# Where the operands of the matrix multiplications of a twelve-stage network begin in SBUF: multiples of 256 bytes for the moving ones, 64 past a multiple of 128 for the weights

## The chip, the cores and the metric

The kernel runs on one core of one Trainium2 chip. The metric is the time of one execution on the device in microseconds (us). Before the change the median of three runs is 1823.18 us (1822.3 to 1828.89).

## The reference, cut to what matters

Two small networks run one after the other on one sequence of 256 tokens of width 1024 (the first adds 16 tokens ahead, which gives 272 columns). Every stage is, in the main, `h @ w` with a large float32 weight matrix `w` that is used once:

```python
h = h + diff_attention(rms_norm(h, da_norm[j]), da_w_qkv[j], ...)      # 1024x3072, 1024x1024
h = h + conv_ffn(rms_norm(h, ffn_norm[i]), ffn_w_up[i], ...)           # 1024x5632, 2816x1024
h = h + dsa_attention(rms_norm(h, dsa_norm[j]), dsa_w_in[j], ...)      # 1024x3656, 1024x1024
...
def swiglu(h, w_gate, w_up, w_down):                                   # 1024x2816 twice, 2816x1024
    return (jax.nn.silu(h @ w_gate) * (h @ w_up)) @ w_down
```

Four such swiglu layers, a gated linear recurrence, a latent attention and two small gated embeddings make up the second network.

## The kernel before, in words

The activations lie transposed in SBUF: 1024 channels are 8 tiles of 128 partitions, and the tokens are the columns. A weight matrix is cut into blocks of 128 x 128, stored in HBM in the order of use, and read once: `load_weights` (L290) brings 16 blocks, 1 MB, in one DMA on SP's queue into one of three `raw` buffers.

A product must keep float32's precision, so every operand is split in two float32r parts, `h` (rounded) and `l` (the rest), and a block is multiplied three times (`mm3`, L336): L338 multiplies the activations' `h` by the weights' `h`, L339 `h` by the weights' `l`, L340 `l` by the weights' `h`. Eight blocks are split at a time by `weight` (L315) or, in the convolution stages, by `groups` (L798): ACT rounds `raw` into `wh` (L326, L815), DVE subtracts into `wl`. These tiles come from the pool `spl`, four buffers each.

In almost all products the block of weights is the stationary operand (loaded by an LDWEIGHTS instruction) and the activations are the moving one, with 272 columns (stage da, conv0 and most of dsa), 258 (the rest of dsa, conv1's first product) or 256 (all that follows). In a few (`proj_n`, L373) it is the other way round: the weights move, 512 columns wide, and 128 columns of the activations are loaded.

The moving operands are tiles of one row of 8 or 22 blocks per partition. `operand` (L488) makes most of them (`xh` and `xl` from the pool `res`, `hh` and `hl` between the two products of a feed-forward layer). The attention stages have `oh` and `ol`, the recurrence `mof`, `mok`, `moml` and `mob`, the latent attention `ch`, `cl` and the tiles `q0` to `q7` and `c0` to `c7`.

Where these begin in a partition follows from the order in which the pools lay them out. In the program that is built from the kernel before:

| tiles | columns | bytes past a multiple of 256 |
|---|---|---|
| all `wh`, `wl` (8 buffers, 4096 bytes apart) | | 64 |
| `xh`, `xl` of every stage, block 0 | 272, 258, 256 | 160 |
| the same, blocks 1 to 7, 272 columns (1088 bytes a block) | 272 | 224, 32, 96, 160, ... |
| the same, 258 columns (1032 bytes a block) | 258 | 168, 176, ... 216 |
| the same, 256 columns (1024 bytes a block) | 256 | 160 |
| `oh`, `ol` of da; `hh`, `hl` of conv0 (1088 bytes a block) | 272 | 0, 64, 128, 192 in turn |
| `hh`, `hl` of conv1, glu00, glu01, glu10; `ph`, `pl` of ple0 | 256 | 128 |
| `hh`, `hl` of glu11 | 256 | 192 |
| `mof`, `mok`, `mob`; `moml`; `ch`, `cl` | 256 | 64; 128; 96 |

The stages run in this order, and their two products follow each other on TensorE without a break: da 7 to 165 us, conv0 165 to 372, dsa 372 to 554, conv1 554 to 746, glu00 746 to 943, even 943 to 1071, glu01 1071 to 1259, ple0 1259 to 1301, glu10 1301 to 1493, mla 1493 to 1598, glu11 1598 to 1788, ple1 to the end. In a feed-forward stage the first two thirds multiply `xh`, `xl`, the last third `hh`, `hl`.

The order of the instructions on each engine is planned by the framework from priorities (`EARLIER`, L195); in the convolution stages and in dsa's attention it is written out by hand.

Of the kernel before, what the change touches and what calls it, by code (L numbers as in the profile page):

```python
# [9 lines left out]
F32 = mybir.dt.float32  # L10
F32R = mybir.dt.float32r
# [9 lines left out]
TA = 272  # L21
TB = 256

NQ = NM - 2
TQ = TA - NQ
KD = 8
FT = 22
G = 16
GS = 8
# [152 lines left out]

TAGS = {"ru": "t0", "s": "t0", "rv": "t1", "z": "t1", "d": "t1", "ra": "t2", "rb_": "t2", "vt": "t3", "sq": "t4",
# [21 lines left out]
def part(f):  # L205

    @wraps(f)
    def moved(self, *a, **k):
        with self.earlier(f.__name__):
            return f(self, *a, **k)  # L210
    return moved


class Net:
# [36 lines left out]
    def t_(self, shape, dt=F32, tag="t", pool=None):  # L251
        self.nt += 1
        pool = pool or self.tmp
        name = f"{tag}_{self.nt}"
        if pool is self.tmp:
            tag = TAGS.get(tag, tag)
        bufs = {"bufs": BUFS[tag]} if pool is self.tmp and tag in BUFS else {}
        return pool.tile(shape, dt, name=name, tag=tag, **bufs)
# [55 lines left out]

    @part  # L315
    def weight(self, n=1):
        nc = self.nc
        i = self.pos % G
        if i == 0:
            self.load_weights()  # L320
        if i in self.cuts:
            self.at, g = i, min(self.cuts[i], self.left)
            raw = self.raw[:, i * 128:(i + g) * 128]
            h = self.t_([128, GS * 128], F32R, "wh", self.spl)
            l = self.t_([128, GS * 128], F32R, "wl", self.spl)
            nc.scalar.copy(out=h[:, :g * 128], in_=raw)  # L326
            self.tt(l[:, :g * 128], raw, h[:, :g * 128].bitcast(F32), OP.subtract)
            self.cur = (h, l)
        self.pos += n
        self.left -= n  # L330
        s = slice((i - self.at) * 128, (i - self.at + n) * 128)
        if i + n == G:
            self.cuts = {j: GS for j in range(0, G, GS)}
        return self.cur[0][:, s], self.cur[1][:, s]
# [153 lines left out]
    def operand(self, kt, T, tag="x", pool=None):  # L488

        ts = [self.t_([128, kt, T], F32R, tag + c, pool or self.res) for c in "hl"]  # L490
        return [[t[:, k] for k in range(kt)] for t in ts]
# [141 lines left out]
    def diff_attention(self, scope):  # L633
# [35 lines left out]
        o = [pool.tile([128, KD, TA], F32R, name=n) for n in ("oh", "ol")]  # L669
# [134 lines left out]
    def groups(self, key):  # L804

        self.begin(key)
        n = self.left
        for i in range(0, n, GS):
# [4 lines left out]
            h = self.t_([128, GS * 128], F32R, "wh", self.spl)  # L813
            l = self.t_([128, GS * 128], F32R, "wl", self.spl)
# [97 lines left out]
    def dsa(self, scope):  # L912
# [19 lines left out]
        o = [pool.tile([128, KD, TQ], F32R, name=n) for n in ("oh", "ol")]  # L932
# [11 lines left out]
        rk = self.t_([128, TA], F32, "rk")  # L944
# [7 lines left out]
        kn = self.t_([128, TA], F32, "kn")  # L952
        ks = self.t_([128, TA], F32, "ks")
# [19 lines left out]
        def index(i):  # L973
            q0, qn = QT[i + 1]
            nk = q0 + qn
            sc = pool.tile([128, TA], F32, name=f"sc{i}")[:, :nk]
            for h in range(8):
# [5 lines left out]
                else:  # L983
                    rl = self.t_([128, TA], F32, "rl")[:, :nk]
# [345 lines left out]
    def even(self, scope):  # L1330
# [5 lines left out]
        big = lambda n, dt=F32: pool.tile([128, W], dt, name=n)  # L1336
# [187 lines left out]
        for part, tags in zip(mo, (("f", "k"), ("ml", "b"))):  # L1524
            for tag in tags:
                t = pool.tile([128, 4, TB], F32R, name=f"mo{tag}", tag=tag)
                part += [t[:, i] for i in range(4)]
# [73 lines left out]
    def mla(self, scope):  # L1601
# [26 lines left out]
        for m, p in enumerate(self.projs(x, KD, TB, 6, 3)):  # L1628
            self.section("c")
            t = self.t_([128, TB], F32, f"c{m}", pool)  # L1630
# [117 lines left out]
        def queries(h):  # L1748
# [5 lines left out]
            qT[h] = self.t_([128, TB], F32, f"q{h}", pool)  # L1754
# [54 lines left out]
        def outputs(h, aT):  # L1809
# [5 lines left out]
            o[0].append(self.t_([128, TB], F32R, f"q{h}", pool))  # L1815
            o[1].append(self.t_([128, TB], F32R, f"c{h}", pool))
# [124 lines left out]
```

## Time and profile before

| | |
|---|---|
| median of 3 runs | 1823.18 us |
| the profiled execution: its time, its span | 1823.16 us, 1821.4 us |
| busy share of the span: PE, DVE, ACT, POOL | 98%, 70%, 53%, 17% |
| mean granted clock of TensorE | 0.988 of full speed |
| DMA | 296 MB, 162 GB/s on average |

PE is TensorE, PEld its weight loads, DVE VectorE, ACT ScalarE, POOL GpSimd. The span is the time from the first to the last instruction of the profiled execution. A matmul's record lasts about 0.28 us, and the next one begins long before its end, so PE shows as busy throughout; what a matmul costs in a row of equal ones is the distance from one start to the next, called its pitch here. From a table of stretches it is (length + 0.28 us) / count, as every record that reaches into the stretch is counted.

### The profile page before, as it was taken

How to read it: one execution, taken by the hardware profiler on the slowest of the kernel's cores; microseconds unless marked ns; L12 is line 12 of the kernel's file. 1: busy time of each engine (PE TensorE's matmuls, PEld its weight loads, DVE VectorE, ACT ScalarE, POOL GpSimd, SP SyncE). 2: the span in 40 equal slices, each digit the busy share in tenths (PEclk: the TensorE clock that was granted, in tenths of full speed). 3: DMA queues.
4: the chain of work that ended last, by engine and by line, in shares of the span. 5: the costliest groups of instructions: out<-in, count | busy, mean ns of one | idle time of the engine just before them, and what ended most of it. 6: DMA issues, size and time to landing. Idle time of an engine off the chain costs nothing.

```text
span 1821.4 us, 34478 instructions
## 1 busy us (share of the span) xinstructions
PE 1780.2 (98%) x13982; PEld 1698.2 (93%) x13982; DVE 1283.1 (70%) x2294; ACT 964.8 (53%) x1664; POOL 303.9 (17%) x301
## 2 busy tenths in 40 slices
PE   8999999999999999999999999999899999999998
PEld 7889999998779999899997799999899998899997
DVE  7776887578567986666678876666866679676666
ACT  4444877433356875444446554445554447654444
POOL 1202443112103441300013210001300014000001
PEclk9999999999899999999999999999999999999999
DMA  7323355454304555455554245555355553255552
GB/s 242 120 101 139 140 185 186 169 183 159 130 27 160 186 187 191 155 186 185 185 200 149 96 174 185 186 185 191 139 182 185 184 186 122 94 192 180 180 184 87
DMA packets 51151, 295.90 MB, mean 162 GB/s; under 512 B 6832, under 2 KB 15152, under 8 KB 16688
## 3 DMA queue, kind: packets, MB, share of 16 engines
q1 hardware_dynamic: 50992, 293.70, 45.6%
q8 instruction: 110, 1.80, 0.4%
q14 instruction: 49, 0.40, 0.1%
HBM read 287.56 MB, written 1.05 MB: 158 GB/s over the span
## 4 chain that ended last, share of the span: by engine, by line
PE 92%; DVE 3%; POOL 2%; ACT 2%; issue 1%; DMA 0%; SPq 0%; DVEq 0%; ACTq 0%; POOLq 0%
PE acc L338 27%; PE acc L340 27%; PE acc L339 27%; PE t L504 2%; PE s L588 1%; PE s L1432 1%; DVE wl L249 1%; POOL sacc L249 1%; POOL lv L249 1%; PE s L1786 1%; PE s L980 0%; PE o L620 0%; PE s L339 0%; PE t L478 0%; PE s L340 0%
## 5 line engine op out<-in xcount | busy, mean ns | idle before, releaser
L249 DVE TENSOR_TENSOR wl<-raw,wh 128x1024 fp32r<-128x1024 f32 (+1 forms) x541 | 677.1, 1253 | 263.2 <-ACT wh L326 255.8
L326 ACT CAST wh<-raw 128x1024 fp32r<-128x1024 f32 (+1 forms) x453 | 473.1, 1046 | 579.4 <-PE acc L340 392.8
L339 PE MATMUL acc<-xh,wl 128*128 128x256 f32 (+2 forms) x2632 | 751.9, 286 | 5.2 <-DVE wl L249 5.1
L338 PE MATMUL acc<-xh,wh 128*128 128x256 f32 (+2 forms) x2632 | 754.4, 287 | 2.6 <-ACT xh L395 2.3
L340 PE MATMUL acc<-xl,wh 128*128 128x256 f32 (+2 forms) x2632 | 753.6, 287 | 0.0
L338 PEld LDWEIGHTS acc<-xh,wh 128*128 128x128 f32 x2632 | 499.7, 190 | 7.5 <-ACT xh L395 3.0
L339 PEld LDWEIGHTS acc<-xh,wl 128*128 128x128 f32 x2632 | 499.3, 190 | 7.3 <-DVE wl L249 6.1
L340 PEld LDWEIGHTS acc<-xl,wh 128*128 128x128 f32 x2632 | 497.3, 189 | 1.1 <-DVE xl L396 0.4
L340 PE MATMUL acc<-hl,wh 128*128 128x256 f32 (+1 forms) x1056 | 296.6, 281 | 0.0
L339 PE MATMUL acc<-hh,wl 128*128 128x256 f32 (+1 forms) x1056 | 296.3, 281 | 0.0
L338 PE MATMUL acc<-hh,wh 128*128 128x256 f32 (+1 forms) x1056 | 296.1, 280 | 0.0
L249 POOL TENSOR_TENSOR sacc<-sacc,sq 128x256 f32<-128x256 f32 (+2 forms) x96 | 99.0, 1032 | 1109.5 <-ACT sq L445 1071.3
L338 PEld LDWEIGHTS acc<-hh,wh 128*128 128x128 f32 x1056 | 198.5, 188 | 0.0
L340 PEld LDWEIGHTS acc<-hl,wh 128*128 128x128 f32 x1056 | 198.3, 188 | 0.0
L339 PEld LDWEIGHTS acc<-hh,wl 128*128 128x128 f32 x1056 | 198.3, 188 | 0.0
L249 POOL TENSOR_TENSOR y<-y,z 128x272 f32<-128x272 f32 (+1 forms) x88 | 109.5, 1244 | 162.8 <-ACT z L866 161.6
L815 ACT CAST wh<-raw 128x1024 fp32r<-128x1024 f32 x88 | 91.3, 1038 | 20.2 <-PE acc L340 20.2
L864 ACT ACTIVATE y<-u,cols 128x272 f32<-128x272 f32 (+1 forms) x88 | 53.5, 608 | 53.7 <-DVE u L249 53.4
L249 DVE TENSOR_TENSOR s<-s,acc 128x256 f32<-128x256 f32 x88 | 36.7, 421 | 46.8 <-PE acc L340 45.6
L396 DVE SCALAR_TENSOR_TENSOR xl<-x,cols,xh 128x256 fp32r<-128x256 f32 (+2 forms) x80 | 64.0, 808 | 6.8 <-ACT xh L395 6.8
L395 ACT ACTIVATE xh<-x,cols 128x256 fp32r<-128x256 f32 (+2 forms) x80 | 39.9, 507 | 29.1 <-DVE x L249 28.6
L249 DVE TENSOR_TENSOR hl<-s,hh 128x256 fp32r<-128x256 f32 (+1 forms) x132 | 55.2, 421 | 0.0
(504 smaller groups left out, 2195.3 us busy)
## 6 DMA issues: line engine op xcount, KB each, us to landing
raw<-wts SPq DMA_DIRECT2D x268, 1024.0 KB, 4.8
x<-xT SPq DMA_DIRECT2D x8, 136.0 KB, 4.4
k<-ra SPq DMA_DIRECT2D x16, 68.0 KB, 2.0
raw<-wts SPq DMA_DIRECT2D x2, 512.0 KB, 4.8
out<-xn SPq DMA_DIRECT2D x4, 256.0 KB, 2.0
raw<-wts SPq DMA_DIRECT2D x3, 256.0 KB, 3.6
q<-ra SPq DMA_DIRECT2D x8, 68.0 KB, 2.1
q<-ra SPq DMA_DIRECT2D x8, 64.5 KB, 2.0
```

What stands on the lines that cost most here:

```text
L249: (eng or self.nc.vector).tensor_tensor(out=out, in0=a, in1=b, op=op)
L326: nc.scalar.copy(out=h[:, :g * 128], in_=raw)
L338: mm(out, a[0], b[0], start=first, stop=False)
L339: mm(out, a[1], b[0], start=False, stop=False)
L340: mm(out, a[0], b[1], start=False, stop=last)
L395: nc.scalar.mul(out=h, in_=src, mul=scale)
L396: nc.vector.scalar_tensor_tensor(out=l, in0=src, scalar=scale, in1=h.bitcast(F32), op0=OP.mult, op1=OP.subtract)
L504: self.nc.tensor.transpose(out, in_, self.ident[:n, :n])
L588: self.nc.tensor.matmul(out, q[ps, q0:q0 + qn], k[ps, :q0 + qn], start=True, stop=False)
L815: self.nc.scalar.copy(out=h, in_=raw)
L864: nc.scalar.activation(out=y, in_=u[:, 2:], func=AF.Identity, scale=tap(n, 2), bias=self.col("conv_b", 44 * layer + 22 * (n % 2) + n // 2))
L1432: nc.tensor.matmul(p[:, i], ke[:, c], qe[:, c], start=True, stop=True)
```

## The change

It adds a constant `LINE = 256` and places the tiles by it. The tiles of moving activations begin on a multiple of 256 bytes, and the blocks in them are padded to a multiple of 256 bytes: with 272 or 258 columns a block takes 1280 bytes in place of 1088 or 1032, with 256 it stays at 1024. The weight tiles get 16 unused columns ahead of their 1024, and an alignment of 128 bytes, so that the data begin 64 bytes past a multiple of 128. In dsa four small tiles (`rk`, `kn`, `ks`, `rl`) move from the shared pool `tmp` to pools of the stage; `rk` and `ks` share the buffers of the score tiles `sc0` and `sc1`. The instructions, their number and their sizes stay.

In dsa some products begin inside a block (`off` in `projs`, L351): the index heads at column 16, the queries at column 14. Those columns keep their distance of 64 and 56 bytes from the block's start. The 512 wide moving operands of `proj_n` are weights and lie where those lie.

```diff
+LINE = 256
...
+def lines(n):
+
+    return -(-n * 4 // LINE) * LINE // 4
...
-    def t_(self, shape, dt=F32, tag="t", pool=None):
+    def t_(self, shape, dt=F32, tag="t", pool=None, line=None):
...
+        if line:
+            bufs["align_bytes"] = line
         return pool.tile(shape, dt, name=name, tag=tag, **bufs)
...
+    def halves(self):
+
+        q = LINE // 16
+        return [self.t_([128, q + GS * 128], F32R, "w" + c, self.spl, LINE // 2)[:, q:] for c in "hl"]
+
...
-            h = self.t_([128, GS * 128], F32R, "wh", self.spl)
-            l = self.t_([128, GS * 128], F32R, "wl", self.spl)
+            h, l = self.halves()
...
-        ts = [self.t_([128, kt, T], F32R, tag + c, pool or self.res) for c in "hl"]
-        return [[t[:, k] for k in range(kt)] for t in ts]
+        ts = [self.t_([128, kt, lines(T)], F32R, tag + c, pool or self.res, LINE) for c in "hl"]
+        return [[t[:, k, :T] for k in range(kt)] for t in ts]
...
-        o = [pool.tile([128, KD, TA], F32R, name=n) for n in ("oh", "ol")]
+        o = [pool.tile([128, KD, lines(TA)], F32R, name=n, align_bytes=LINE)[:, :, :TA] for n in ("oh", "ol")]
...
-        rk = self.t_([128, TA], F32, "rk")
+        rk = pool.tile([128, TA], F32, name="rk", tag="sc0")
...
-        kn = self.t_([128, TA], F32, "kn")
-        ks = self.t_([128, TA], F32, "ks")
+        kn = pool.tile([128, TA], F32, name="kn")
+        ks = pool.tile([128, TA], F32, name="ks", tag="sc1")
...
-            sc = pool.tile([128, TA], F32, name=f"sc{i}")[:, :nk]
+            sc = pool.tile([128, TA], F32, name=f"sc{i}", tag=f"sc{i}")[:, :nk]
...
-                    rl = self.t_([128, TA], F32, "rl")[:, :nk]
+                    rl = self.t_([128, TA], F32, "rl", wk)[:, :nk]
...
-        big = lambda n, dt=F32: pool.tile([128, W], dt, name=n)
+        big = lambda n, dt=F32: pool.tile([128, W], dt, name=n, align_bytes=LINE)
...
-                t = pool.tile([128, 4, TB], F32R, name=f"mo{tag}", tag=tag)
+                t = pool.tile([128, 4, TB], F32R, name=f"mo{tag}", tag=tag, align_bytes=LINE)
...
-            o[0].append(self.t_([128, TB], F32R, f"q{h}", pool))
-            o[1].append(self.t_([128, TB], F32R, f"c{h}", pool))
+            o[0].append(self.t_([128, TB], F32R, f"q{h}", pool, LINE))
+            o[1].append(self.t_([128, TB], F32R, f"c{h}", pool, LINE))
```

The tiles `oh`, `ol` of dsa change as those of da do, `c0` to `c5` and `q0` to `q7` of the latent attention as the last lines shown, and `groups` calls `halves` as `weight` does.

## Rows read from the trace of the kernel before

**Rows 1.** The page, part 1: busy time of each engine.

```profile
PE 1780.2 (98%) x13982; PEld 1698.2 (93%) x13982; DVE 1283.1 (70%) x2294; ACT 964.8 (53%) x1664; POOL 303.9 (17%) x301
```

**Rows 2.** The page, part 4: the chain that ended last, by engine, by line.

```profile
PE 92%; DVE 3%; POOL 2%; ACT 2%; issue 1%; DMA 0%; SPq 0%; DVEq 0%; ACTq 0%; POOLq 0%
PE acc L338 27%; PE acc L340 27%; PE acc L339 27%; PE t L504 2%; PE s L588 1%; PE s L1432 1%; DVE wl L249 1%; POOL sacc L249 1%; POOL lv L249 1%; PE s L1786 1%; PE s L980 0%; PE o L620 0%; PE s L339 0%; PE t L478 0%; PE s L340 0%
```

**Rows 3.** PE's groups by form: line, op, tiles, form, count, busy us, mean ns.

```profile
L338 PE MATMUL acc<-xh,wh 128*128 128x256 f32 x1560 | 441.4, 283 | 2.3 <-ACT xh L395 2.3
L338 PE MATMUL acc<-hh,wh 128*128 128x256 f32 x880 | 245.6, 279 | 0.0
...
L338 PE MATMUL acc<-xh,wh 128*128 128x272 f32 x656 | 194.5, 297 | 0.3 <-ACT le L659 0.3
...
L338 PE MATMUL acc<-xh,wh 128*128 128x258 f32 x416 | 118.5, 285 | 0.0
...
L338 PE MATMUL acc<-hh,wh 128*128 128x272 f32 x176 | 50.5, 287 | 0.0
L338 PE MATMUL acc<-wh,xh 128*128 128x512 f32 x96 | 39.2, 409 | 0.0
...
L338 PE MATMUL acc<-oh,wh 128*128 128x272 f32 x64 | 18.7, 292 | 0.0
...
L338 PE MATMUL acc<-oh,wh 128*128 128x258 f32 x64 | 18.4, 287 | 0.0
...
L338 PE MATMUL s<-xh,wh 128*128 128x256 f32 x40 | 11.4, 286 | 0.0
...
L338 PE MATMUL s<-xh,wh 128*128 128x272 f32 x24 | 7.2, 319 | 2.7 <-ACT wh L326 2.7
```

**Rows 4.** Table of stretches in which TensorE has one kind of product.

```profile
core 0: us, PE busy (x) PEld busy (x) DVE busy (x) ACT busy (x) POOL busy (x), PEclk, DMA share, GB/s
235.00:285.00 50.00, 50.00 (x401) 50.00 (x400) 40.15 (x68) 38.46 (x68) 25.05 (x17) 1.00 0.53 187
310.00:370.00 60.00, 60.00 (x480) 60.00 (x480) 32.65 (x36) 26.84 (x35) 6.83 (x6) 1.00 0.47 168
640.00:680.00 40.00, 40.00 (x333) 40.00 (x333) 32.52 (x56) 30.78 (x55) 18.65 (x14) 1.00 0.52 180
690.00:744.00 54.00, 54.00 (x461) 54.00 (x460) 30.58 (x35) 25.82 (x35) 6.04 (x6) 1.00 0.52 186
...
1080.00:1195.00 115.00, 115.00 (x959) 114.95 (x959) 74.39 (x111) 56.35 (x83) 0.00 (x0) 1.00 0.52 184
1202.00:1258.00 56.00, 56.00 (x497) 56.00 (x496) 35.48 (x42) 26.97 (x35) 6.83 (x6) 1.00 0.54 191
...
1433.00:1490.00 57.00, 57.00 (x486) 57.00 (x485) 35.12 (x43) 26.04 (x34) 7.11 (x6) 1.00 0.53 185
...
1728.00:1786.00 58.00, 58.00 (x491) 58.00 (x491) 35.06 (x42) 26.50 (x35) 6.12 (x6) 1.00 0.52 182
```

**Rows 5.** PE in order of time where glu01 passes from xh to hh.

```profile
1198.06 0.28 PE L340 MATMUL acc<-xl,wh 128*128 128x256 f32 x1
...
1198.90 0.28 PE L338 MATMUL acc<-hh,wh 128*128 128x256 f32 x1
...
1199.47 0.28 PE L340 MATMUL acc<-hl,wh 128*128 128x256 f32 x1
```

**Rows 6.** What PE waited for, longest first.

```profile
PE t L478 <- DVE dg L249: 6.5, 3, 2.8
```

**Rows 7.** The page, part 5: how the weights are split.

```profile
L249 DVE TENSOR_TENSOR wl<-raw,wh 128x1024 fp32r<-128x1024 f32 (+1 forms) x541 | 677.1, 1253 | 263.2 <-ACT wh L326 255.8
L326 ACT CAST wh<-raw 128x1024 fp32r<-128x1024 f32 (+1 forms) x453 | 473.1, 1046 | 579.4 <-PE acc L340 392.8
```

**Rows 8.** The instructions of dsa's tiles rk and sc.

```profile
L955 DVE SCALAR_TENSOR_TENSOR kn<-ki,cols,rk x1: 494/494/494, 394.7 to 394.7; 64x272 f32<-64x272 f32 x1
...
L982 DVE TENSOR_SCALAR sc<-s,wi x2: 367/434/501, 405.2 to 428.8; 128x144 f32<-128x144 f32 x1, 128x272 f32<-128x272 f32 x1
```

More of the change, by code (lines that the diff above doesn't have):

```diff
@@ L812, in groups @@
             raw = self.raw[:, i % G * 128:(i % G + GS) * 128]
-            h = self.t_([128, GS * 128], F32R, "wh", self.spl)
-            l = self.t_([128, GS * 128], F32R, "wl", self.spl)
+            h, l = self.halves()
             self.nc.scalar.copy(out=h, in_=raw)
@@ L931, in dsa @@
         vn = pool.tile([128, 3, 1024], F32, name="vn")
-        o = [pool.tile([128, KD, TQ], F32R, name=n) for n in ("oh", "ol")]
+        o = [pool.tile([128, KD, lines(TQ)], F32R, name=n, align_bytes=LINE)[:, :, :TQ] for n in ("oh", "ol")]
         self.section()
@@ L1629, in mla @@
             self.section("c")
-            t = self.t_([128, TB], F32, f"c{m}", pool)
+            t = self.t_([128, TB], F32, f"c{m}", pool, LINE)
             self.tt(t, p, r, OP.mult)
@@ L1753, in queries @@
                 pss[g] = self.sps([128, 2, 4])
-            qT[h] = self.t_([128, TB], F32, f"q{h}", pool)
+            qT[h] = self.t_([128, TB], F32, f"q{h}", pool, LINE)
             nc.vector.tensor_copy(out=qT[h], in_=p)
```

## The prediction, made before the changed kernel was run

> **What bounds the kernel.** I read the busy times first: PE is busy 98% of the span, DVE 70%, ACT 53% [rows 1]. The chain that ended last says the same in another way: 92% of it is PE, and 81% is the three lines of `mm3` [rows 2]. The longest wait of PE on another engine is 6.5 us in total [rows 6]. So the time is the number of matmuls times the pitch from one to the next, and a change counts only by what it does to the pitch.
>
> Next, how many there are [rows 3]. Each row stands for one line of `mm3` and so for a third. 256 columns: 1560 + 40 and 16 more in mla's lead tile, 1616 a line or 4848 on `xh`, `xl`; 880 a line or 2640 on `hh`, `hl`; by the plan of weights another 168 a line or 504 in the small groups (`ev_o` 64, `ml_o` 64, `pp0` 16, 24 of `ml_n`). 272 columns: 656 + 176 + 64 + 24 = 920 a line, 2760. 258 columns: 480 a line, 1440. 512 columns: 96 a line and a few more, where the weights move.
>
> Then the pitch, from stretches with a single kind of product [rows 4], as (length + 0.28) / count. With 256 columns on `xh`, 160 bytes past a multiple of 256: 115.28 / 959 = 120.2 ns. On `hh` at 128 bytes: conv1 54.28 / 461 = 117.7, glu10 57.28 / 486 = 117.9, but glu01 56.28 / 497 = 113.2. On `hh` at 192 bytes, glu11: 58.28 / 491 = 118.7. With 272 columns: 125.4 on conv0's `xh`, at odd multiples of 32 bytes, and 125.6 on its `hh`, which runs through 0, 64, 128 and 192. With 258 columns and steps of 8 bytes: 121.0. These rows have a granted clock of 1.00, which is the higher level, 2.4 GHz, so the clock explains none of the differences; nor does a wait, as PE has no idle time in any of them. Instruction, shape and weights' offset (64 past a multiple of 128) are the same. What differs is where the moving operand begins, and in glu01 against glu10 not even that (both at 128): two pitches exist for one placement. At the seam inside glu01 it can be seen to switch: seven steps on `xh` take 0.84 us, 120 ns each, the next five on `hh` 0.57 us, 114 each [rows 5].
>
> **The change, part by part.** *Weights.* They lie 64 past a multiple of 128 before and after, so this part removes nothing; the larger tiles only make half of them 192 in place of 64 past a multiple of 256. No row has that. Bounds: nothing, or the 1.0 ns between 117.7 and the 118.7 of glu11, where moving operand and weights differ by 128 bytes instead of 64; I take nothing.
>
> *256 columns on `xh`.* From 160 to 0 past 256. No row shows 0 with 256 columns; the nearest are those at 128, which are whole multiples of 128 too: 113.2 at one end, 117.8 at the other. All rows at 128 but one are at the upper end, but those came in from a stage at 160, and glu01 stayed at the lower one for all its stretch. I can't tell which of the two a stage takes, so I take half: 115.5. 4848 x (120.2 - 115.5) = 22.8 us. (The 96 of dsa's index heads begin 64 past a multiple of 256 after the change too; they are 0.4 us of it.) A loss is the last rival below.
>
> *256 columns on `hh`.* From 128 to 0: 1584 (conv1, glu00, glu10) x (117.8 - 115.5) = 3.6 us; glu01 loses 528 x (115.5 - 113.2) = 1.2; glu11 gains 528 x (118.7 - 115.5) = 1.7. Together 4.1.
>
> *The 504 others.* No clean stretch of them; between nothing and the 4.6 ns from 117.8 to 113.2. At half, 1.2 us.
>
> *272 columns.* Padding puts every block at 0. Priced by columns: 115.5 x 272 / 256 = 122.7, against 125.5 now: 2760 x 2.8 = 7.7 us; bounds 120.3 (from 113.2) and 125.2 (from 117.8).
>
> *258 columns.* 115.5 x 258 / 256 = 116.4 against 121.0, for 1248, as 192 (dsa's queries, from column 14) stay 56 bytes past: 5.7 us. Bounds 114.1 and 118.7.
>
> *512 columns.* The moving side stays at 64 past 128: nothing, either way at most the 4.6 ns per 256 columns, 3 us.
>
> *dsa's four tiles.* `rk` now shares a buffer with `sc0`, so the first write to `sc0` waits for the last reader of `rk`. That reader starts at 394.7, that write at 405.2 [rows 8]: 10 us of cover. Were it gone, DVE would stand 0.5 us, and ACT's `rl` and POOL's select behind it. `ks` and `sc1` have 30 us. `rl` keeps two buffers. Nothing. No DMA and no queue is moved.
>
> *The other engines.* DVE and ACT write the same elements; no row says that their 1253 and 1046 ns [rows 7] depend on the place, so nothing. They hide behind PE: in glu01's first product DVE works 74.4 of 115 us, and if PE needs 110 it is at 67%. What is late next is DVE in conv0's first product, 40.2 of 50 us [rows 4], 84% at the fastest pitch.
>
> Sum: 22.8 + 4.1 + 1.2 + 7.7 + 5.7 = 41.5 us. PE is 92% of the chain [rows 2], the rest isn't shortened: 38 us. The profiled execution took 1823.2 us (span 1821.4), 0.02 from the median, so **1785**.
>
> **The rivals.**
> *All fall into the fast pitch.* 113.2, 120.3 and 114.1: 4848 x 7.0 + 1584 x 4.6 + 528 x 5.5 + 504 x 4.6 + 2760 x 5.2 + 1248 x 6.9 = 33.9 + 7.3 + 2.9 + 2.3 + 14.4 + 8.6 = 69 us, at 92% 64: 1759. For it: glu01, and that now all operands lie alike, so that nothing throws a stage out of it. Against: three of four stages at 128.
>
> *All take the slower aligned pitch.* 117.8, 125.2, 118.7: 4848 x 2.4 - 528 x 4.6 + 528 x 0.9 + 2760 x 0.3 + 1248 x 2.3 = 11.6 - 2.4 + 0.5 + 0.8 + 2.9 = 13.4, at 92% 12: 1811. For it: the same three rows.
>
> *The place doesn't matter.* The pitches would then be those of how the stages happen to start, and come out as now, 1823. Against: every clean stretch on `xh` has 120, every one at 128 less. The Trainium skill (SBUF — State Buffer, "Who interferes with whom") says that PE waits on nobody and reads moving operand and weights through two independent ports; by it this change does nothing, and 1823 is its time. The trace speaks against a pitch that nothing but the width sets: 113.2, 117.8 and 120.2 for one form [rows 4].
>
> *Slower: 0 collides.* A moving operand at 0 may meet weights at 64 and 192 alternately, and never settle; every 256-wide matmul then costs the 120.2 of `xh`, and 272 columns 127.7 by columns. The xh groups stay, `hh` loses 1584 x 2.4 + 528 x 7.0 + 528 x 1.5 = 8.3, the others 504 x 2.4 = 1.2, the 272 wide 2760 x 2.2 = 6.1: 15.6, at 92% 14: 1837. It decides from a mean pitch that is 0.8 ns above today's over some 12,000 matmuls (9 us). For it: with 272 columns the tiles at 0, 64, 128 and 192 are no better than those at 32 [rows 4].
>
> **How the numbers follow.** The middle course 0.34, all fast 0.28, all slower-aligned 0.16, no effect 0.14, slower 0.08. Half a per cent, 9 us, is about what a measurement of this kernel can tell from no change. Faster by more: the first two and three quarters of the third, 0.74; within: 0.18; slower: 0.08. The range goes from the all fast case to the slower-aligned one with a few us at each end for the 512 wide and the unknown place of weights: 1755 to 1816.
>
> **What would show it.** The stretches on `xh` in glu00 to glu11: 120.2 now, 113 to 118 if I am right, one value for a whole stage. The stretches on `hh` should no longer differ from `xh` of the same stage. conv0 should go from 125.5 to 120 to 123. The counts, DVE's and ACT's means and PE's waits should stay. Wrong it would be if `xh` stays at 120, or if PE's idle time grows by what its pitch saves.

## The result, and the profile after

The changed kernel takes 1783.9 us (median of 5 runs, 1783.2 to 1787.12); the kernel before, timed beside it, 1826.32 us (5 runs, 1822.3 to 1828.89). The ratio is 0.9774, 95% interval 0.9755 to 0.9793. Executions of one kernel differ by up to some 14 us, the longer ones at a lower mean granted clock (the change run once more: 1779.2 us at 0.989, 1793.5 at 0.981). The profiled execution has a span of 1782.2 us against 1821.4, so 39.2 us less. 1785 had been predicted; how the terms fared is another matter.

Parts 1 and 4 of the page of the kernel after: busy times, and the chain that ended last by engine and by line.

```profile
PE 1739.4 (98%) x13982; PEld 1658.8 (93%) x13982; DVE 1282.5 (72%) x2294; ACT 964.3 (54%) x1664; POOL 300.7 (17%) x301
...
PE 90%; DVE 4%; POOL 2%; ACT 2%; issue 1%; DMA 0%; SPq 0%; DVEq 0%; ACTq 0%; POOLq 0%
PE acc L352 26%; PE acc L353 26%; PE acc L354 26%; PE t L518 2%; DVE wl L257 1%; PE s L602 1%; PE s L1445 1%; POOL sacc L257 1%; PE s L1799 1%; POOL lv L257 1%; PE s L993 0%; PE o L634 0%; PE s L353 0%; PE s L354 0%; PE s L1798 0%
```

Against [rows 1, 2]: as many instructions on every engine, and PE is the one whose busy time falls by much, 1780.2 to 1739.4. The chain still belongs to `mm3`, which is now L352 to L354.

The table of stretches of the kernel after, in the order conv0 `xh`, conv0 `hh`, conv1 `xh`, conv1 `hh`, glu01 `xh`, glu01 `hh`, glu11 `xh`, glu11 `hh`. The clean stretches have moved up with the stages, so they aren't those of [rows 4] to the microsecond.

```profile
core 0: us, PE busy (x) PEld busy (x) DVE busy (x) ACT busy (x) POOL busy (x), PEclk, DMA share, GB/s
235.00:285.00 50.00, 50.00 (x402) 50.00 (x401) 40.57 (x68) 38.86 (x68) 24.90 (x17) 1.00 0.51 182
310.00:370.00 60.00, 60.00 (x482) 60.00 (x482) 33.16 (x37) 26.79 (x36) 6.89 (x7) 1.00 0.48 169
640.00:680.00 40.00, 40.00 (x334) 40.00 (x333) 33.13 (x57) 30.94 (x55) 18.03 (x14) 1.00 0.51 179
690.00:740.00 50.00, 50.00 (x444) 50.00 (x443) 29.85 (x33) 24.53 (x33) 6.08 (x6) 1.00 0.56 196
...
1072.00:1175.00 103.00, 103.00 (x911) 103.00 (x910) 70.37 (x99) 53.66 (x80) 0.00 (x0) 1.00 0.54 193
1183.00:1238.00 55.00, 55.00 (x488) 55.00 (x487) 35.01 (x42) 26.30 (x35) 6.52 (x6) 1.00 0.55 192
...
1575.00:1685.00 110.00, 110.00 (x971) 109.95 (x970) 74.56 (x109) 56.87 (x83) 0.00 (x0) 1.00 0.55 193
1695.00:1745.00 50.00, 50.00 (x444) 50.00 (x443) 32.35 (x39) 24.28 (x33) 5.50 (x6) 1.00 0.56 197
```

With 256 columns all have one pitch. The second products of conv1 and glu11 have 50.28 / 444 = 113.2 ns, before 117.7 and 118.7; glu01's second has 55.28 / 488 = 113.3, before 113.2; glu01's first has 103.28 / 911 = 113.4, before 120.2. The 110.28 / 971 = 113.6 of glu11's first takes in a short gap at 1578 us. With 272 columns next to nothing has changed: 50.28 / 402 = 125.1 and 60.28 / 482 = 125.1, for 125.4 and 125.6. With 258 columns nothing: 40.28 / 334 = 120.6 for 121.0. The granted clock is 1.00 in all of them, before and after.

PE in order of time at the seam inside glu01, as in [rows 5], but after:

```profile
1180.02 0.28 PE L352 MATMUL acc<-xh,wh 128*128 128x256 f32 x1
...
1180.36 0.28 PE L352 MATMUL acc<-hh,wh 128*128 128x256 f32 x1
...
1180.93 0.28 PE L354 MATMUL acc<-hl,wh 128*128 128x256 f32 x1
```

Three steps on `xh` take 0.34 us and five on `hh` 0.57: 113 and 114 ns. The switch from 120 to 114 that stood there is gone.

What stayed, as [rows 6, 7] (waits of PE, part 5 of the page):

```profile
PE t L492 <- DVE dg L257: 7.0, 3, 2.9
...
L257 DVE TENSOR_TENSOR wl<-raw,wh 128x1024 fp32r<-128x1024 f32 (+1 forms) x541 | 676.6, 1252 | 250.3 <-ACT wh L340 243.2
L340 ACT CAST wh<-raw 128x1024 fp32r<-128x1024 f32 (+1 forms) x453 | 473.0, 1046 | 537.5 <-PE acc L354 364.3
```

The splitting of the weights costs 1252 and 1046 ns as before, and PE's longest wait is 7.0 us for 6.5.

Summed over the whole trace, from each matmul's start to the next one's, by the width of the first (summed over all 13,981 distances; the pitch is the mean without the gaps at seams):

| columns | matmuls | before, us | after, us | pitch before, after, ns |
|---|---|---|---|---|
| 256 | 7,992 | 964.9 | 924.2 | 118.9, 113.6 |
| 272 | 2,760 | 376.8 | 377.4 | 125.4, 125.1 |
| 258 | 1,440 | 176.4 | 176.3 | 120.5, 120.5 |
| 512 | 378 | 103.4 | 104.6 | 233.9, 231.1 |
| others | 1,411 | 190.2 | 189.9 | |

The products of 256 columns save 40.7 us; all else together gives back 1.4, so 39.3 in all, the span's 39.2.

### The profile page after: what moved, and what is told of

The parts are those of the page before. It is cut to its first block, busy times and chain, and to the rows that moved or that the text cites. A ratio compares the mean times of both kernels' runs of the same rounds, so it can differ in the third digit from the quotient of the medians.

```text
span 1782.2 us, 34479 instructions
## 1 busy us (share of the span) xinstructions
PE 1739.4 (98%) x13982; PEld 1658.8 (93%) x13982; DVE 1282.5 (72%) x2294; ACT 964.3 (54%) x1664; POOL 300.7 (17%) x301
## 4 chain that ended last, share of the span: by engine, by line
PE 90%; DVE 4%; POOL 2%; ACT 2%; issue 1%; DMA 0%; SPq 0%; DVEq 0%; ACTq 0%; POOLq 0%
PE acc L352 26%; PE acc L353 26%; PE acc L354 26%; PE t L518 2%; DVE wl L257 1%; PE s L602 1%; PE s L1445 1%; POOL sacc L257 1%; PE s L1799 1%; POOL lv L257 1%; PE s L993 0%; PE o L634 0%; PE s L353 0%; PE s L354 0%; PE s L1798 0%
## 5 line engine op out<-in xcount | busy, mean ns | idle before, releaser
L257 DVE TENSOR_TENSOR wl<-raw,wh 128x1024 fp32r<-128x1024 f32 (+1 forms) x541 | 676.6, 1252 | 250.3 <-ACT wh L340 243.2
L340 ACT CAST wh<-raw 128x1024 fp32r<-128x1024 f32 (+1 forms) x453 | 473.0, 1046 | 537.5 <-PE acc L354 364.3
L352 PE MATMUL acc<-xh,wh 128*128 128x256 f32 (+2 forms) x2632 | 747.1, 284 | 2.9 <-ACT xh L409 2.6
L354 PE MATMUL acc<-xl,wh 128*128 128x256 f32 (+2 forms) x2632 | 744.2, 283 | 0.0
L352 PEld LDWEIGHTS acc<-xh,wh 128*128 128x128 f32 x2632 | 499.9, 190 | 7.4 <-ACT xh L409 3.0
L354 PEld LDWEIGHTS acc<-xl,wh 128*128 128x128 f32 x2632 | 498.7, 190 | 0.8
L352 PE MATMUL acc<-hh,wh 128*128 128x256 f32 (+1 forms) x1056 | 293.9, 278 | 0.0
L354 PE MATMUL acc<-hl,wh 128*128 128x256 f32 (+1 forms) x1056 | 293.6, 278 | 0.0
L352 PEld LDWEIGHTS acc<-hh,wh 128*128 128x128 f32 x1056 | 198.6, 188 | 0.0
L354 PEld LDWEIGHTS acc<-hl,wh 128*128 128x128 f32 x1056 | 198.3, 188 | 0.0
```

The source lines that it names most:

```text
L257: (eng or self.nc.vector).tensor_tensor(out=out, in0=a, in1=b, op=op)
L352: mm(out, a[0], b[0], start=first, stop=False)
L354: mm(out, a[0], b[1], start=False, stop=last)
```

## The experiments

Two questions: why does every product of 256 columns now have 113.3 ns, and why did those of 272 and 258 not move? The first theory was the prediction's own: a moving operand on a multiple of 128 or 256 bytes can have either of two pitches, whatever the weights. Its rivals: the distance from weights to moving operand decides; the history decides, that is, a stage keeps the pitch in which it starts. Pitches below are those of a clean stretch at clock 1.00; the columns of all tables are those of the one above. Places are bytes past a multiple of 256.

One fact of the changed program belongs here. With 64 bytes ahead of the data a weight buffer is 4224 bytes instead of 4096, so four buffers begin in turn at 64 and at 192. Before, all began at 64.

### Many places, weights as in the change

`operand` gets an offset by stage:

```diff
+OFF = {('conv1', 'h'): 128, ('glu00', 'x'): 128, ('glu00', 'h'): 64, ('glu01', 'x'): 64, ('glu01', 'h'): 192,
+       ('glu10', 'x'): 32, ('glu10', 'h'): 160, ('glu11', 'x'): 16, ('glu11', 'h'): 96}
-        ts = [self.t_([128, kt, lines(T)], F32R, tag + c, pool or self.res, LINE) for c in "hl"]
-        return [[t[:, k, :T] for k in range(kt)] for t in ts]
+        q, n = OFF.get((self.stage, tag), 0) // 4, lines(T)
+        ts = [self.t_([128, kt * n + q], F32R, tag + c, pool or self.res, LINE) for c in "hl"]
+        return [[t[:, q + k * n:q + k * n + T] for k in range(kt)] for t in ts]
```

> The changed kernel, with the moving operands of single products pushed off their multiple of 256 bytes, weights as in the change (64 or 192 past). conv1's hh at 128 and glu00's xh at 128; glu00's hh and glu01's xh at 64; glu01's hh at 192; glu10's xh at 32 and its hh at 160; glu11's xh at 16 and its hh at 96. Theory 'place against weights' (whole multiples of 128 don't meet weights at 64 past 128): 113 ns at 128 as at 0, about 118.7 at 64 and 192 as in glu11 before, about 120 at 32, 160, 96 and 16. Theory 'multiples of 256 alone': 113 nowhere but at 0, 117.8 at 128. Theory 'history' (a stage of whole multiples of 64 takes either pitch, as the one before left it): no order by place, 113 or 118 at 128, 64 and 192 alike.

One run, 1816.5 us. Stretches of conv1 `hh` (128), glu00 `hh` (64), glu01 `hh` (192), glu11 `xh` (16):

```profile
690.00:740.00 50.00, 50.00 (x443) 50.00 (x443) 29.50 (x33) 24.52 (x33) 6.08 (x6) 1.00 0.54 191
...
875.00:932.00 57.00, 57.00 (x481) 57.00 (x480) 34.75 (x41) 25.82 (x35) 6.16 (x6) 1.00 0.52 185
...
1190.00:1248.00 58.00, 58.00 (x489) 58.00 (x488) 35.65 (x43) 26.00 (x34) 6.08 (x6) 1.00 0.51 182
...
1600.00:1715.00 115.00, 115.00 (x968) 114.95 (x968) 74.27 (x107) 56.59 (x84) 0.00 (x0) 1.00 0.52 184
```

128 has 113.5 ns, as 0 has; 64 has 119.1, 192 119.2, 16 119.1. By the same reading 32 and 160 have 119.2 and 119.1, and 96 has 118.1. So a change of place within the pair 0 and 128 costs nothing, everything else 5 to 6 ns. That 64 and 192, whole multiples of 64, are as bad as 16 speaks for a relation to the weights, which lie at just these two places. A stage that follows a slow one was fast again where its place was 0, so history alone doesn't decide here.

### Many places, all weights at 0

```diff
-        q = LINE // 16
-        return [self.t_([128, q + GS * 128], F32R, "w" + c, self.spl, LINE // 2)[:, q:] for c in "hl"]
+        return [self.t_([128, GS * 128], F32R, "w" + c, self.spl, LINE) for c in "hl"]
...
+OFF = {('conv1', 'h'): 64, ('glu00', 'h'): 64, ('glu01', 'x'): 64, ('glu10', 'x'): 128, ('glu10', 'h'): 192,
+       ('glu11', 'x'): 32, ('glu11', 'h'): 96}
...
```

Here and in the runs below with an `OFF`, `operand` takes the offsets as in the first run.

> The weights' part undone and set the other way: all weights on a multiple of 256, moving operands at 0 (glu00's xh, glu01's hh, all of even, ple, mla), 64 (conv1's hh, glu00's hh, glu01's xh), 128 (glu10's xh), 192 (glu10's hh), 32 and 96 (glu11). Theory 'difference' (only the distance between moving operand and weights counts, 64 past 128 is good): the moving operands at 64 and 192 have 113 ns, those at 0 and 128 some 118.7. Theory 'the weights' place doesn't count': 113 at 0 as after the change, the rest as in the run with weights at 64. In both, 120 at 32 and 96.

One run, 1816.23 us. conv1 `hh` (64), glu01 `hh` (0), glu10 `hh` (192):

```profile
690.00:740.00 50.00, 50.00 (x427) 50.00 (x426) 28.62 (x32) 23.59 (x33) 6.01 (x6) 1.00 0.53 190
...
1195.00:1250.00 55.00, 55.00 (x461) 55.00 (x460) 33.30 (x40) 24.38 (x32) 5.39 (x5) 1.00 0.50 175
...
1432.00:1485.00 53.00, 53.00 (x470) 53.00 (x469) 34.34 (x41) 25.04 (x33) 7.10 (x6) 1.00 0.55 197
```

0 over weights at 0 is now among the worst, 55.28 / 461 = 119.9; 64 has 117.8, and 192 has 113.4. By the same reading 128 has 118.8, 32 has 116.9 and 96 has 120.2. The very place that the change gives to every moving tile is among the worst with other weights: the theory that the place of the moving operand alone decides is out. But the distance alone isn't enough: weights at 64 or 192 and moving at 0 are 192 or 64 apart, and here 192 apart is fast, 64 apart is not.

### Other widths at the place of the change

The two products of the four swiglu layers at widths of 240 to 320, each beginning at 0, weights as in the change. Wider ones read on into the next block, and what lies beyond 256 is dropped; glu11 computes only the first 240 tokens.

```diff
+WIDE = {"00": (272, 288), "01": (258, 264), "10": (320, 304), "11": (240, 240)}
...
-        ps = self.projs(x, KD, TB, 2 * FT, 4)
+        ps = (p[:, :N] for p in self.projs(self.wide(x, WIDE[key][0]), KD, WIDE[key][0], 2 * FT, 4))
...
-            p = self.proj(h, FT, TB)
+            p = self.proj(self.wide(h, WIDE[key][1]), FT, WIDE[key][1])[:, :N]
```

> All places as in the change; only the number of moving columns differs: glu00 272 on xh and 288 on hh, glu01 258 and 264, glu10 320 and 304, glu11 240 and 240 (the surplus columns come from the next block and are dropped, the last block repeats the one before it; in glu11 the last 16 tokens are left out of the layer). Theory 'so much a column' (0.443 ns a column, as 113.3 for 256): 240 at 106, 258 at 114, 264 at 117, 272 at 120, 288 at 127.5, 304 at 134.6, 320 at 141.7; then conv0's 125 would come from something else in that stage. Theory 'width must be a multiple of 64 columns (256 bytes)': 320 at 141.7, the others dear, 0.461 to 0.467 ns a column: 258 at 120.5, 272 at 125, 288 at 133, 304 at 141. Theory 'multiple of 16 columns': 240, 272, 288, 304, 320 at 0.443, 258 and 264 dear.

One run, 1863.68 us. 272, 258, 264, 320 and 240 columns:

```profile
770.00:880.00 110.00, 110.00 (x882) 110.00 (x881) 67.77 (x97) 50.61 (x76) 0.00 (x0) 1.00 0.50 174
...
1082.00:1203.00 121.00, 121.00 (x1008) 120.94 (x1007) 78.55 (x118) 58.91 (x87) 0.19 (x1) 1.00 0.53 186
1210.00:1268.00 58.00, 58.00 (x484) 58.00 (x483) 34.76 (x41) 26.13 (x35) 6.78 (x6) 1.00 0.51 182
1330.00:1465.00 135.00, 135.00 (x929) 134.95 (x928) 72.87 (x103) 54.39 (x82) 0.00 (x0) 1.00 0.42 149
...
1655.00:1765.00 110.00, 110.00 (x982) 109.95 (x981) 74.92 (x114) 55.94 (x83) 0.00 (x0) 1.00 0.56 198
```

| columns | 240 | 256 (in the change) | 258 | 264 | 272 | 288 | 304 | 320 |
|---|---|---|---|---|---|---|---|---|
| pitch, ns | 112.3 | 113.2 to 113.6 | 120.3 | 120.4 | 125.0 | 131.8 | 139.6 | 145.6 |
| columns at 2.4 GHz, ns | 100.0 | 106.7 | 107.5 | 110.0 | 113.3 | 120.0 | 126.7 | 133.3 |
| above that | 12.3 | 6.6 to 6.9 | 12.8 | 10.4 | 11.7 | 11.8 | 12.9 | 12.3 |

From 240 to 320 columns a column costs (145.6 - 112.3) / 80 = 0.416 ns, one period of 2.4 GHz. The second line is width / 2.4, the third the difference. Seven widths pay 10 to 13 ns over their columns and 256 alone pays 7, at the same place and over the same weights. At its slow pitches, 117.8 to 120.0, 256 columns pay 11 to 13 as well. None of the theories had this: of the eight widths only 256 has the cheap pitch here, and two columns more cost 7 ns. Whether 240, 264, 288, 304 or 320 columns have a cheap pitch at other places was not run; 272 and 258 had none at any of the places that were run (about 125 and 119 ns at best).

### Everything at 128

```diff
+OFF = {('conv1', 'h'): 128, ('glu00', 'x'): 128, ('glu00', 'h'): 128, ('glu01', 'x'): 128, ('glu01', 'h'): 128,
...
```

> All moving operands of 256 columns that the helper makes (xh, hh, ph, ch) at 128 past a multiple of 256, as hh was before; the rest as in the change. Theory 'place against weights': as fast as the change, 1784. Theory 'multiples of 256 alone': the 7,500 matmuls cost 117.8 in place of 113.5, 1784 + 32 = 1816. Theory 'history' (the xh at 160 ahead threw the stages on hh out of the fast pitch): 1784 too, with single stages at 117.8 possible.

1786.05 us (4 runs, 1783.8 to 1788.39), ratio to before 0.9794 (0.9778 to 0.981). glu01 `xh`:

```profile
1065.00:1175.00 110.00, 110.00 (x970) 109.85 (x968) 76.40 (x114) 56.75 (x84) 0.00 (x0) 1.00 0.55 195
```

110.28 / 970 = 113.7 ns, and the intervals overlap with the change's. With weights by turns at 64 and 192, a multiple of 128 does as well as one of 256.

### The change without its weights

```diff
-        q = LINE // 16
-        return [self.t_([128, q + GS * 128], F32R, "w" + c, self.spl, LINE // 2)[:, q:] for c in "hl"]
+        return [self.t_([128, GS * 128], F32R, "w" + c, self.spl) for c in "hl"]
```

In this program the plain weight tiles come to lie at 0.

> The weights' part undone, the moving operands as in the change: plain tiles of 4096 bytes, which then lie on multiples of 256 (all at 0). By the run with weights at 0 each matmul of 256 columns costs 120.0 ns, and the time is 1784 + 7,900 x (120.0 - 113.6) = 1834, slower than before (1822). Theory 'the moving operands alone bring it': 1784.

1832.82 us (5 runs, 1831.14 to 1836.14), ratio 1.0046 (1.0028 to 1.0063). conv1 `hh`, glu01 `xh`:

```profile
690.00:740.00 50.00, 50.00 (x419) 50.00 (x419) 27.22 (x32) 23.61 (x31) 4.83 (x5) 1.00 0.52 184
...
1075.00:1185.00 110.00, 110.00 (x918) 109.95 (x917) 72.01 (x108) 53.68 (x81) 0.99 (x1) 1.00 0.54 188
```

50.28 / 419 = 120.0 and 120.1 ns, and by the same reading 119.9 in glu00's second product: everything at the slow end. The aligned and padded moving operands by themselves make the kernel slower than before, by 0.3 to 0.6%.

### The weights alone

Weights as in the change; `xh`, `hh`, `ph` and `ch` back to the places of before (160, 128 or 192, 128, 96), and no padding. The recurrence's tiles, `q` and `c` stay as in the change.

```diff
-    return -(-n * 4 // LINE) * LINE // 4
+    return n
...
+OFF = {('glu00', 'x'): 160, ('glu01', 'x'): 160, ('glu10', 'x'): 160, ('glu11', 'x'): 160, ('conv1', 'h'): 128,
+       ('glu00', 'h'): 128, ('glu01', 'h'): 128, ('glu10', 'h'): 128, ('glu11', 'h'): 192,
...
```

> The weights' part alone: weights at 64 and 192 by turns, moving operands where they lay before (xh at 160, hh at 128, in glu11 192, ph 128, ch 96, no padding); mo, q and c as in the change. Theory 'the turns': hh at 128 goes to 113.4 in conv1, glu00 and glu10 (1584 x 4.4 = 7 us), xh at 160 to 119.2 (4848 x 0.9 = 4 us), some 1 us in the small groups: about 1810. Theory 'history': hh stays at 117.8 behind xh at 160, about 1817. Theory 'the moving operands alone bring it': 1822.

1815.71 us (10 runs, 1807.21 to 1822.0), ratio 0.9948 (0.9928 to 0.9968). glu00 `hh` (128), glu01 `xh` (160):

```profile
880.00:935.00 55.00, 55.00 (x487) 55.00 (x486) 34.85 (x42) 26.28 (x35) 6.20 (x6) 1.00 0.55 192
1070.00:1188.00 118.00, 118.00 (x991) 117.95 (x990) 78.17 (x118) 58.34 (x86) 0.00 (x0) 1.00 0.53 187
```

`hh` at 128 has 55.28 / 487 = 113.5 right behind an `xh` at 160 with 119.4. In the kernel before, conv1 and glu10 had 117.7 and 117.9 for the same `hh` at the same place, behind the same `xh` [rows 4]. All four products of `hh` at 128 were fast here, conv1, glu01 and glu10 at 113.5, 113.4 and 113.8. What differs is that half of the weights lie at 192. So with weights by turns a slow stage ahead doesn't hold the next one at the slow pitch: there the theory of history falls. Whether it falls with one place for all weights too, this run can't tell.

### All weights at 64

One place for all weights, several for the moving tiles, no padding:

```diff
+OFF = {('glu01', 'x'): 128, ('glu01', 'h'): 128, ('glu10', 'x'): 160, ('glu10', 'h'): 128, ('glu11', 'h'): 128}
...
-    return -(-n * 4 // LINE) * LINE // 4
+    return n
...
-        return [self.t_([128, q + GS * 128], F32R, "w" + c, self.spl, LINE // 2)[:, q:] for c in "hl"]
+        return [self.t_([128, q + GS * 128 + 48], F32R, "w" + c, self.spl, LINE)[:, q:q + GS * 128] for c in "hl"]
```

> All eight weight tiles at 64 past a multiple of 256, as before the change, in place of 64 and 192 by turns; blocks of 272 and 258 columns without padding; moving operands at 0 on conv1's hh, all of glu00, even and glu11's xh, at 128 on glu01's xh and hh, at 160 then 128 in glu10 (the order of before), at 0 then 128 in glu11. Theory 'the turns' (64 and 192 in turn lead every stage into the fast pitch; with all at 64 a stage can stay in the slow one): 117.8 on most of the stages at 0 or 128, whatever stood ahead. Theory 'history': 113.4 in all of them but glu10's hh, which follows operands at 160 and stays at 117.8. Theory 'distance by 256' (64 behind the weights is good, 64 ahead is not): 113.4 on all at 0, 117.8 on all at 128.

One run, 1810.99 us. glu00 `hh` (0), glu01 `hh` (128), glu11 `xh` (0):

```profile
880.00:928.00 48.00, 48.00 (x426) 48.00 (x426) 31.38 (x37) 22.96 (x32) 6.19 (x6) 1.00 0.55 195
...
1188.00:1243.00 55.00, 55.00 (x470) 55.00 (x469) 34.60 (x41) 24.93 (x33) 6.09 (x6) 1.00 0.54 189
1600.00:1712.00 112.00, 112.00 (x953) 112.00 (x952) 73.51 (x105) 54.93 (x83) 0.00 (x0) 1.00 0.54 187
```

At 0, 48.28 / 426 = 113.3 in glu00 but 112.28 / 953 = 117.8 in glu11: two pitches for one placement in one run, as in the kernel before. At 128, 117.6.

### Few columns loaded

If the slow pitch comes from the reading of the moving operand meeting the loading of the next weights, a shorter load should cost less. In the second products of the swiglu layers only the first 64, 64, 32 and 128 output channels of each block of 128 are computed, the rest is left out.

```diff
+LOADED = {"00": 64, "01": 64, "10": 32, "11": 128}
+OFF = {('glu00', 'h'): 64, ('glu01', 'x'): 64, ('glu10', 'h'): 64, ('glu11', 'x'): 64, ('glu11', 'h'): 64}
...
-            self.mm3(p[:, :T], self.weight(), (x[0][k], x[1][k]), k == 0, k == kt - 1)
+            self.mm3(p[:M, :T], [w[:, :M] for w in self.weight()], (x[0][k], x[1][k]), k == 0, k == kt - 1)
...
```

> Weights as in the change; in the second product of the swiglu layers only a part of the 128 weight columns is loaded (glu00 and glu01 64, glu10 32, glu11 all 128), so the rest of the layer's output is left out. Moving operands at 64 on xh of glu01 and glu11 and on hh of glu00, glu10 and glu11, at 0 on hh of glu01. Theory 'the moving read meets the load of the next weights': fewer columns loaded, fewer meetings, so glu00's hh (at 64, 64 columns loaded) falls from 119.2 to between 113 and 116, glu10's (32) further, glu01's (at 0) stays at or below 113; glu11's stays at 119.2. Theory 'the moving operand's place alone' (its own reads cost more at 64): 119.2 in glu00, glu10 and glu11 alike, 113.4 in glu01.

One run, 1798.17 us. glu00 `hh` (at 64, 64 loaded), glu01 `hh` (at 0, 64 loaded), glu10 `hh` (at 64, 32 loaded, its first part and the rest), glu11 `hh` (at 64, 128 loaded):

```profile
875.00:930.00 55.00, 55.00 (x478) 55.00 (x477) 34.39 (x41) 25.81 (x34) 6.17 (x6) 1.00 0.53 189
1188.00:1243.00 55.00, 55.00 (x488) 55.00 (x486) 34.87 (x42) 26.29 (x35) 6.52 (x6) 1.00 0.55 192
1412.00:1421.00 9.00, 9.00 (x79) 8.30 (x77) 5.26 (x8) 3.86 (x5) 0.00 (x0) 1.00 0.51 172
1423.00:1468.00 45.00, 45.00 (x399) 42.82 (x398) 29.53 (x35) 21.35 (x29) 7.08 (x6) 1.00 0.53 188
1704.00:1760.00 56.00, 56.00 (x474) 56.00 (x474) 33.96 (x41) 25.81 (x34) 6.11 (x6) 1.00 0.53 189
```

At 64: 118.7 ns with 128 columns loaded and 115.6 with 64. With 32 the stage has two pitches, 9.28 / 79 = 117.5 in its first 11 us and 45.28 / 399 = 113.5 from there to its end, which is that of a good place. At 0 with 64 loaded 113.3, the same as with 128. So the floor of 113.3 doesn't depend on the load, and what a bad place adds, 5.4 and 2.3 ns and with 32 in the end nothing, falls with the columns loaded. The moving operand's own reads are the same in the three stages, so they alone don't set it; a meeting with the load of the weights would fit. A matmul with fewer loaded columns also writes fewer partitions of PSUM. At 0 that changes nothing, but at 64 the two were not told apart.

### The change without its padding

```diff
-    return -(-n * 4 // LINE) * LINE // 4
+    return n
```

> The change without the padding of the 272 and 258 column blocks (1088 and 1032 bytes apart again, block 0 at 0 past 256); weights by turns at 64 and 192 and all 256-column tiles at 0, as in the change. 'Only products of 256 columns have a cheap pitch': conv0 stays at 125 ns, conv1's first product at 120.5, the 256-column stages at 113.4, and the time is the change's, 1784 us within 2. 'The padding is worth its columns' (the prediction's terms for 272 and 258, 13.4 us at 92%): 12 us slower than the change, 1796.

1784.06 us (4 runs, 1782.2 to 1788.1), ratio to before 0.977 (0.9741 to 0.9798). Beside it the change itself, once more:

> The kernel after once more, unchanged, beside the one without padding on the same chip: 1784 us by every theory; it is the base for that comparison.

1780.79 us (5 runs, 1779.22 to 1793.49), ratio 0.9751 (0.9721 to 0.978). Without padding, conv0 `xh`, conv0 `hh`, conv1 `xh`:

```profile
235.00:285.00 50.00, 50.00 (x401) 50.00 (x401) 39.97 (x67) 38.20 (x68) 24.91 (x17) 1.00 0.53 189
310.00:370.00 60.00, 60.00 (x480) 60.00 (x480) 32.69 (x37) 26.80 (x35) 6.81 (x6) 1.00 0.48 169
640.00:680.00 40.00, 40.00 (x337) 40.00 (x336) 33.13 (x57) 31.79 (x57) 18.70 (x14) 1.00 0.56 187
```

125.4, 125.6 and 119.5 ns, with padding 125.1, 125.1 and 120.6. Over 2,760 and 1,440 matmuls that is about 1 us for the padding and 1.5 against it. The intervals of the two ratios overlap: the padding brings nothing that can be told. The version without it is as fast and takes less SBUF, 1088 or 1032 bytes a block instead of 1280.

### One place for all weights, once more, and the other one

The version without padding, weight buffers 4352 bytes apart, all at 64 in one run (`q = 16`) and all at 192 in the other (`q = 48`):

```diff
-        q = LINE // 16
-        return [self.t_([128, q + GS * 128], F32R, "w" + c, self.spl, LINE // 2)[:, q:] for c in "hl"]
+        q = 16
+        return [self.t_([128, GS * 128 + 64], F32R, "w" + c, self.spl, LINE)[:, q:q + GS * 128] for c in "hl"]
```

> As the version without padding, every 256-column tile at 0 past 256, but the weights' buffers 4352 bytes apart, so that all begin 64 past a multiple of 256. 'The turns of 64 and 192 make the cheap pitch sure': with one place alone each stage takes 113.4 or 117.8 ns, as stages of equal places did in the kernel before and in the run with all weights at 64; all at 117.8 would cost 7,992 x 4.4 = 35 us, about half of that is likely: 1790 to 1815. 'The distance from weights to the moving tile decides' (moving 192 past the weights): all stages at 113.4, 1784.

1793.34 us (4 runs, 1790.76 to 1794.66), ratio 0.9834 (0.9819 to 0.9848). glu01 `xh`, glu01 `hh`, glu11 `xh`, all at 0:

```profile
1070.00:1180.00 110.00, 110.00 (x971) 109.95 (x970) 75.94 (x116) 56.46 (x84) 0.00 (x0) 1.00 0.54 192
1190.00:1240.00 50.00, 50.00 (x444) 50.00 (x442) 32.67 (x40) 24.26 (x33) 6.58 (x6) 1.00 0.55 190
...
1580.00:1690.00 110.00, 110.00 (x934) 109.95 (x934) 71.96 (x101) 54.76 (x81) 0.00 (x0) 1.00 0.53 188
```

113.6 and 113.2, but 110.28 / 934 = 118.1 in glu11.

> The same with all weights 192 past a multiple of 256 and the moving tiles at 0. 'The turns make the cheap pitch sure': again each stage 113.4 or 117.8, 1790 to 1815. 'The distance decides': the moving tile lies 64 past the weights, as with hh at 128 over weights at 64, which had 117.8 in three of four stages before: all stages at 117.8, 1819.

1814.36 us (5 runs, 1806.6 to 1822.51), ratio 0.9942 (0.9918 to 0.9966). glu01 `xh`, glu11 `hh`:

```profile
1080.00:1190.00 110.00, 110.00 (x934) 109.95 (x934) 72.80 (x108) 54.97 (x81) 0.00 (x0) 1.00 0.53 185
...
1730.00:1785.00 55.00, 55.00 (x470) 55.00 (x469) 34.32 (x41) 24.95 (x34) 6.13 (x6) 1.00 0.54 189
```

118.1 and 117.6; every stage is slow. With one place for all weights each theory takes one run: the moving tile 64 past the weights was slow throughout, as the theory of distance had it, and 192 past them mostly fast but not in glu11, which the distance can't explain.

Counted over the nine long products of 256 columns (conv1's second and two in each swiglu layer), pitches under 114 as fast and 117 to 119 as slow:

| weights | moving tile | fast | slow | from |
|---|---|---|---|---|
| by turns at 64 and 192 | 0 or 128 | 42 | 0 | change, both its runs; all at 128; no padding (nine each); many places (2); weights alone (4) |
| one place | 192 past the weights | 11 | 3 | all weights at 64 (3 and 1; 7 and 2), all at 0 (1 and 0) |
| one place | 64 past the weights | 1 | 19 | before (1 and 3), all at 64 (0 and 4), at 192 (0 and 9), at 0 (0 and 3) |
| one place | as the weights | 0 | 11 (at 120) | the change without its weights (9), all at 0 (2) |

Other distances agree between places: 96 past the weights has 120.2 over weights at 64 ([rows 4], `xh` of glu01) and at 0, 128 past them 118.7 and 118.8. With one place, then, the distance orders the pitches as far as they were run, with exceptions at 64 and 192 alone.

What the change does is the combination: moving tiles at 0 or 128, and weights that begin by turns 64 and 192 past. One place can go either way at 64 and 192; with turns none of 42 was slow. The traces show what the turns do. Call a row unbroken if TensorE does nothing in it but products of 256 columns. With all weights at 64 and all moving tiles at 0 there are 21 such rows of 27 to 1560 matmuls, and at clock 1.00 each keeps one pitch from its start to its end, 13 of them 113.3 and 8 of them 117.8. The pitch changes only where other work stands between two rows, here two matmuls of one column (PE in order of time, all weights at 64):

```profile
1574.12 0.28 PE L352 MATMUL acc<-xh,wh 128*128 128x256 f32 x1
...
1575.14 0.28 PE L352 MATMUL acc<-xh,wh 128*128 128x256 f32 x1
...
1575.37 0.28 PE L472 MATMUL t<-ones,sacc 128*128 128x1 f32 x2
...
1576.29 0.28 PE L352 MATMUL acc<-xh,wh 128*128 128x256 f32 x1
...
1579.82 0.28 PE L352 MATMUL acc<-xh,wh 128*128 128x256 f32 x1
```

Nine steps take 1.02 us before it, 113.3 ns each, and 30 steps 3.53 us behind it, 117.7 each; the rest of glu11 keeps that. Here history, in the sense above, does hold. With weights by turns a row can start slow as well, but doesn't stay so. In the change once more, behind a pause of 0.3 us at 1564:

```profile
1565.07 0.28 PE L352 MATMUL acc<-q,wh 128*128 128x256 f32 x1
...
1569.70 0.28 PE L352 MATMUL acc<-q,wh 128*128 128x256 f32 x1
...
1571.12 0.28 PE L352 MATMUL acc<-q,wh 128*128 128x256 f32 x1
...
1572.82 0.28 PE L352 MATMUL acc<-q,wh 128*128 128x256 f32 x1
```

That is 118.7 ns over 39 steps and 113.3 over 15, with nothing but products of 256 columns between. In the two profiles of the change no row goes the other way without a pause, and none is slow for more than 60 matmuls. So with turns a slow row falls into the fast pitch, and with one place it stays where it started. Which pitch a row starts in, and what in the chip the two are, stays open.

## Why the prediction was right, and where it wasn't

**The bound: right.** The time is the number of matmuls times the pitch, and 39.2 us less of span came with 40.8 us less of PE's busy time; no wait grew by more than a microsecond or two.

**256 columns on `xh` and `hh`: the pitch right, its reason half right, the gain mis-sized.** The fast pitch is the one read from the trace, but the place of the moving tiles doesn't bring it alone: without the weights' part every stage had 120. "I can't tell which of the two a stage takes, so I take half: 115.5" was the step that failed: all stages take the fast one. What stood ahead could not tell the stages apart: glu01's `hh`, the fast one, had come in from an `xh` at 160 like the slow ones [rows 5]. On `xh` 4848 x (120.2 - 113.6) = 32.0 us in place of 22.8; on `hh` 1584 x (117.8 - 113.3) = 7.1 for 3.6, nothing for the loss of 1.2 in glu01, 528 x (118.7 - 113.2) = 2.9 for 1.7. That is 42 for 27; the whole trace has 7,992 x (118.9 - 113.6) = 42.4, the small products included, and the rival in which all stages are fast had 33.9 + 7.3 + 2.9 + 2.3 = 46 for these terms.

**The weights: "this part removes nothing", wrong.** Without them the rest of the change costs 0.3 to 0.6% (ratio 1.0046), and they alone bring 0.3 to 0.7%. In the version without padding, one place for all of them gave 1793 and 1814 us in place of 1784. The step took as bounds "nothing, or the 1.0 ns between 117.7 and the 118.7 of glu11", from rows in which all weights lay at one place, and so could not see what two places do together. It was the part of the diff that looked like a by-product, and without it the rest loses.

**272 and 258 columns: wrong.** The step was "Priced by columns: 115.5 x 272 / 256 = 122.7", 7.7 us, and likewise 5.7 for 258. Measured 0.7 us (2,760 x 0.24) and none. The cheap pitch isn't a price per column: 258 at the same place cost 120.3. The row that spoke against it was cited, for the slower rival: 272 columns at 0, 64, 128 and 192 no better than at 32.

**The sum.** Forecast 41.5 x 92% = 38; the profiled span fell by 39.2. Some 14 us too little for the 256 wide, 13 too much for the other two: that 1785 was so close is luck, as two errors cancel, and the likeliest case as described, stages half fast and half slow, isn't what happened.

**512 columns, dsa's tiles, the other engines: right at nothing.** 378 x 2.8 = 1 us on the 512 wide, within the 3; seams took it back. `wl` and `wh` have their means; DVE in conv0's first product is at 40.6 of 50 us, 81%, as that stretch got no shorter.

**The rivals.** *All fast*: its pitch came for 256 columns, its 23 us for 272 and 258 did not. Its reason, that all operands now lie alike, isn't the cause: with all weights at 64 and all tiles at 0 they lay alike too, and glu11 was slow. *All at the slower pitch* is what weights all at 192 give, 117.6 to 118.1 in every stage, at 1814. *Slower: 0 collides*: its 120 ns came in every stage of the change without its weights, 1833 us where the rival had 1837, but not for its reason. There the weights lie at 0 like the moving tiles; the weights at 64 and 192 alternately, which the rival feared, are what makes the slow pitch give way. *The place doesn't matter* is out. The Trainium skill (SBUF — State Buffer, "Who interferes with whom") gives PE two independent read ports, one for the moving operand and one for the weights. The runs disagree: with both tiles' sizes and the clock alike, 113.3 to 120.0 ns by their places alone, and at a bad place 5.4, 2.3 and in the end 0 ns more as 128, 64 and 32 columns are loaded.

## What to carry to other kernels

Where a kernel is a dense row of matmuls that each load new weights, the start addresses of the two operands are worth 4 to 6% of the pitch at 256 float32r columns: moving tiles at 0 or 128 past a multiple of 256 and weight buffers in turn at 64 and 192 was the one combination that was fast in every stage, because with the turns a slow row doesn't last. Change both together: the moving side alone was 0.5% slower than the kernel before. And before a gain is spread over other shapes by their size, measure one of them: two columns more lost it all. The padding can be left out.

## What the runs showed that was not expected

- One width stands out: 256 columns cost 6.6 to 6.9 ns above their columns at 2.4 GHz, seven widths from 240 to 320 cost 10.4 to 12.9. 240 columns are only 1 ns cheaper than 256.
- The same two addresses can give 113.3 or 117.8 ns for a whole stage of some 100 us, with no idle time of PE and clock 1.00, within one execution.
- With one place for all weights the pitch is kept through an unbroken row of up to 1560 matmuls and can change at two matmuls of one column; with turns a slow row became fast within 60 matmuls.
- What a bad pair of places costs falls with the weight columns loaded: 5.4 ns for 128, 2.3 for 64, in the end nothing for 32.
